# Part of the late modulation summed in the opening of a diffusion block, and filter steps ahead of the first projection

## Chip, cores and metric

The kernel runs on one core of a Trainium2 chip. The metric is the device time of one execution in microseconds (us); lower is better. The engines are TensorE (PE, with its weight loads as PEld), VectorE (DVE), ScalarE (ACT), GpSimd (POOL) and SyncE (SP, whose queue issues most DMAs). Each takes its instructions in a fixed order, and waits on semaphores for the others.

## The reference

One layer of a diffusion backbone over 1024 latent tokens of width 1024, with 256 context tokens. What matters here, cut:

```python
mod = jax.nn.silu(c) @ w_ada[i] + b_ada[i]
mod_c = jax.nn.silu(c_ctx) @ w_ada[i] + b_ada[i]
sh1, sc1, g1, sh2, sc2, g2 = jnp.split(mod[:, None, :], N_MOD, axis=-1)
hc = modulate(rmsnorm(xc, norm1_g[i]), csh1, csc1)
k_c, v_c = jnp.split(hc @ w_in[i][:, NA_WIDTH:3 * NA_WIDTH], 2, axis=-1)
h = modulate(rmsnorm(x, norm1_g[i]), sh1, sc1)
q, k, v, hv, hx1, hx2, gna, ghy = jnp.split(h @ w_in[i], IN_SPLITS, axis=-1)
y_na = neighbourhood_attention(to_heads(q), ..., na_rpb[i])
y_hy = hyena_mixer(hv, hx1, hx2, *hy_params)
x = x + g1 * gated_merge(gna, ghy, y_na, y_hy, w_na_o[i], w_hy_o[i], w_out[i])
h2 = modulate(rmsnorm(x, norm2_g[i]), sh2, sc2)
x = x + g2 * swiglu(h2, ffn_w1[i], ffn_w3[i], ffn_w2[i])
return rmsnorm(x, final_g)
```

The modulation has six parts of 1024 columns: 0 and 1 (shift and scale of the first norm) are needed at once, 2 (a gate), 3 and 4 (the second norm) and 5 (the last gate) only much later; those four are "the late modulation". hyena_mixer convolves with filters that a small network of two sine layers makes from the positions alone (hid = sin(freq * (z @ w1 + b1)), the same again with w2, then @ w3 and a decay), so they depend on no activation.

## The kernel before, in words

Everything is fp32. Products that must keep fp32 precision are made of three fast matmuls of operands split into a rounded high part and the rest: names ending in h and l (hTh, hTl, wh, wl). ACT makes the high part and DVE the low one (`split`, L178), so a matmul with hTl waits for DVE.

The kernel runs in stages: the opening, the side phase, attention with the hyena branch's output, the mixing and output projection, and the feed-forward layer's two halves. The change touches the first two.

**The opening** (`opening`, L741, fed by the generator `hidden`, L283). It computes modulation parts 0 and 1 with matmuls on 1 MB blocks (wada, ada_ps), normalizes x, transposes it on PE (hT_ps), modulates it into hT (`chunk`, or the same lines in `hidden`), and multiplies by the v columns of w_in (wv). There are three passes of eight steps: x tiles 0 to 3, x tiles 4 to 7, and the two ctx tiles (hcT). A step takes one 128-row chunk of the contraction for the four (or two) tiles, 12 (or 6) matmuls at L751, and then transposes the chunk that comes two steps later. At a pass's end the banks are copied to vst (L760), on DVE for even tiles and on ACT for odd ones. `chunk` modulates even chunks on ACT and odd ones on DVE (L276). During the second pass the filters' network (`filter_hidden`, L420) runs in two calls: two matmuls (mlp_ps, L435), seven DVE instructions for argument and range reduction (L436 to L441), and a Sin on ACT. Before the first modulation matmul, PE runs WAKE = 8 calls of a dummy matmul (awake_ps, L356).

**The side phase** (`run`, from L1110). Two generators are interleaved by `_merged`, which always takes the one that has used the smallest part of its weight: `side`, of weight SIDE = 496, and `project`, of weight 33, which makes one projection (48 matmuls in_ps of 512 columns, L199) per turn. `side` in turn merges the filters (weight 97) with `ada_rows` (weight 39), and then runs the long convolution. A filter step issues eight small matmuls (filt_ps, L464) into two banks, and DVE multiplies these by a decay (fv, L471); after four steps, a DFT of the filter follows (dft_ps). psf has five banks, so filt_ps comes to wait for the fv of two steps before. The weight split for the next projection (wl, L178) is on DVE too.

`ada_rows` (L999) computes the late modulation without PE: for each of the parts in pairs (3, 4) and (2, 5), each half of 512 columns and each of eight row blocks, it loads 256 KB of w_ada (wal, four buffers) by SP's queue and DVE adds wal times a column of silu(c) to aacc (L1017; the first of eight is a plain multiplication, L1019). Then a matmul with ones sums over the partitions (ar_ps) and DVE adds the bias row (arow). That makes 64 loads and 64 DVE instructions. After the pair (3, 4) the rows are transposed (ada_t) into mod2.

An instruction that isn't pinned (`keep_in_program_order`) can be placed by the scheduler elsewhere in its engine's order; pinned ones keep the order in which they are written.

Of the kernel before, what the change touches and what calls it, by code (L numbers as in the profile page):

```python
# [160 lines left out]
class Block:  # L161
# [258 lines left out]
    def filter_hidden(self, pool, late, psf):  # L420
        nc, a = self.nc, self.a
        hid, w3 = late()
        self.tc.keep_in_program_order(nc.sync.dma_start(w3, a["fw3"]))
# [4 lines left out]
        w1, w2, col = m[0:66, 0:P], m[:, P:2 * P], m[:, 2 * P:]
        for w, src, b, dst in ((w1, z[0:66], 0, z), (w2, z, 1, hid)):
            arg = pool.tile([P, T], F32, tag="farg", name="farg", bufs=1)  # L430
            kf = pool.tile([P, T], F32, tag="fkf", name="fkf", bufs=1)
            for h in range(2):
                sl = slice(h * 512, (h + 1) * 512)
                ps = psf.tile([P, 512], F32, tag="f", name="mlp_ps")
                self.tc.keep_in_program_order(nc.tensor.matmul(ps, w, src[:, sl], start=True, stop=True))  # L435
                nc.vector.tensor_scalar(arg[:, sl], ps, col[:, b:b + 1], col[:, 2:3], op0=ALU.add, op1=ALU.mult)  # L436
            nc.vector.tensor_scalar(kf, arg, 1.0 / TWO_PI, MAGIC, op0=ALU.mult, op1=ALU.add)
            nc.vector.tensor_scalar(kf, kf, MAGIC, None, op0=ALU.subtract)
            nc.vector.scalar_tensor_tensor(arg, kf, -C1, arg, op0=ALU.mult, op1=ALU.add)
            nc.vector.scalar_tensor_tensor(arg, kf, -C2, arg, op0=ALU.mult, op1=ALU.add)  # L440
            nc.vector.tensor_scalar(arg, arg, PI_LO, -PI_LO, op0=ALU.min, op1=ALU.max)  # L441
# [556 lines left out]

    def ada_rows(self, pool, psf):  # L999

        nc, a = self.nc, self.a
# [3 lines left out]
        def sums(r, pair):
            for n, part in enumerate(pair):
                for h in range(2):
                    acc = pool.tile([P, 512], F32, tag="aacc", name="aacc", bufs=2)  # L1010
                    for k in range(8):
                        w = pool.tile([P, 512], F32, tag="wal2", name="wal", bufs=4)
                        at = part * D + 512 * h
                        nc.sync.dma_start(w, a["w_ada"][k, :, at:at + 512])
                        c = self.cs[:, 2 * k:2 * k + 1]
                        if k:
                            nc.vector.scalar_tensor_tensor(acc, w, c, acc, op0=ALU.mult, op1=ALU.add)  # L1017
                        else:
                            nc.vector.tensor_scalar(acc, w, c, None, op0=ALU.mult)  # L1019
                        yield 0.6  # L1020
                    ps = psf.tile([P, 512], F32, tag="f", name="ar_ps")
                    for j in range(2):
                        g = 64 * h + 32 * j
                        nc.tensor.matmul(ps[g:g + 32, 0:256], ones, acc[:, 256 * j:256 * j + 256], start=True,
                                         stop=True, tile_position=(0, g))
                    rs = r[64 * h:64 * h + 64, 256 * n:256 * n + 256]
                    nc.vector.tensor_add(rs, ps[64 * h:64 * h + 64, 0:256], rs)

        for pair in ((3, 4), (2, 5)):
            r = pool.tile([P, 512], F32, tag="arow", name="arow", bufs=1)  # L1030
            nc.gpsimd.memset(r, 0.0)
            for n, part in enumerate(pair):
                for j in range(4):
                    at = part * D + 256 * j
                    nc.gpsimd.dma_start(r[32 * j:32 * j + 1, 256 * n:256 * n + 256], a["b_ada"][0:1, at:at + 256])
            yield from sums(r, pair)
            for n, part in enumerate(pair):
                for j in range(4):
                    nc.gpsimd.dma_start(self.modd[part][0:1, 256 * j:256 * j + 256],
                                        r[32 * j:32 * j + 1, 256 * n:256 * n + 256])  # L1040
            if pair[0] == 3:
                pt = psf.tile([P, 512], F32, tag="f", name="ada_t")
                for j in range(4):
                    nc.tensor.transpose(pt[:, j * P:(j + 1) * P], r[:, j * P:(j + 1) * P], self.ident)
                v = pt.rearrange("p (n h g q) -> p n q g h", n=2, h=2, g=4)[:, :, 0]
                cols = lambda t: t.rearrange("p (g h) -> p g h", h=2)
                nc.vector.tensor_copy(cols(self.mod2[:, 1, :]), v[:, 0])
                nc.vector.scalar_tensor_tensor(cols(self.mod2[:, 0, :]), v[:, 1], 1.0, cols(self.ng[:, 1, :]),
                                               op0=ALU.add, op1=ALU.mult)
# [552 lines left out]
```

## Time and profile before

| what | value |
| --- | --- |
| median of 3 runs | 1702.17 us (1702.06 to 1704.37) |
| profiled execution | 1705.87 us, of which the span is 1704.1 us |
| mean granted TensorE clock | 0.987 |
| opening, 0 to 95.5 us | PE busy 86.53 us |
| side phase, 95.5 to 607 us | PE busy 491.40 of 511.50 us, clock 0.97 |
| attention and hyena output, to 913 us | PE busy 300.93 of 306.00 us |
| mixing, to 1046 us | PE busy 131.96 of 133.00 us |
| feed-forward, to 1704 us | PE busy 644.59 of 658.00 us |

The profile shows one execution. "Busy" is the time in which an engine has an instruction running; what ended an idle stretch is inferred from semaphores. The clock is the share of full speed that was granted to TensorE: at 0.50 the same matmul takes twice as long, and PE still counts as busy. The DMA share is the mean busy share of the core's 16 DMA engines.

### The profile page before, as it was taken

How to read it: one execution, taken by the hardware profiler on the slowest of the kernel's cores; microseconds unless marked ns; L12 is line 12 of the kernel's file. 1: busy time of each engine (PE TensorE's matmuls, PEld its weight loads, DVE VectorE, ACT ScalarE, POOL GpSimd, SP SyncE). 2: the span in 40 equal slices, each digit the busy share in tenths (PEclk: the TensorE clock that was granted, in tenths of full speed). 3: DMA queues.
4: the chain of work that ended last, by engine and by line, in shares of the span. 5: the costliest groups of instructions: out<-in, count | busy, mean ns of one | idle time of the engine just before them, and what ended most of it. 6: DMA issues, size and time to landing. Idle time of an engine off the chain costs nothing.

```text
span 1704.1 us, 22676 instructions
## 1 busy us (share of the span) xinstructions
PE 1655.4 (97%) x8144; PEld 1311.7 (77%) x8144; DVE 1232.1 (72%) x2095; ACT 685.8 (40%) x1202; POOL 149.6 (9%) x271
## 2 busy tenths in 40 slices
PE   8989999999999999999999999999999999999997
PEld 5767766777767787887787887888888888778886
DVE  3756788799988876565865868967865666379477
ACT  6532343313112124555654326733333333355455
POOL 0010020101000022020200001000100111000000
PEclk9989999999999999999999999999999999999999
DMA  9265366554555365344747414333422223394344
GB/s 362 82 216 176 119 211 206 175 180 169 173 173 204 124 201 183 109 148 146 211 155 262 153 62 173 122 126 120 159 101 97 99 103 115 117 386 152 97 120 155
DMA packets 110310, 274.38 MB, mean 161 GB/s; under 512 B 15471, under 2 KB 24563, under 8 KB 107893
## 3 DMA queue, kind: packets, MB, share of 16 engines
q1 hardware_dynamic: 90296, 212.39, 37.2%
q0 software_dynamic: 19104, 60.08, 10.4%
q8 instruction: 65, 1.06, 0.3%
q10 hardware_dynamic: 797, 0.45, 0.1%
q14 instruction: 48, 0.39, 0.1%
HBM read 205.48 MB, written 67.39 MB: 160 GB/s over the span
## 4 chain that ended last, share of the span: by engine, by line
PE 55%; DVE 5%; DMA 4%; ACT 1%; issue 1%; ACTq 0%; DVEq 0%; SPq 0%
PE x_ps L1303 15%; PE z_ps L1303 7%; PE in_ps L199 6%; PE dx_ps L1472 5%; PE out_ps L1241 4%; PE dz_ps L1472 3%; PE hy_ps L199 2%; PE y_ps L1303 2%; PE pt_ps L927 2%; PE pt_ps L913 2%; PE na_ps L199 2%; PE dy_ps L1472 1%; PE s_ps L893 1%; DMA ar<-g 1%; PE s_ps L896 1%
## 5 line engine op out<-in xcount | busy, mean ns | idle before, releaser
L199 PE MATMUL in_ps<-hTh,wl 128*128 128x512 f32 x576 | 236.8, 411 | 5.1 <-ACT proj L697 4.0
L199 PE MATMUL in_ps<-hTl,wh 128*128 128x512 f32 x576 | 230.1, 399 | 0.0
L199 PE MATMUL in_ps<-hTh,wh 128*128 128x512 f32 x576 | 229.9, 399 | 0.0
L199 PEld LDWEIGHTS in_ps<-hTh,wl 128*128 128x128 f32 x576 | 110.3, 192 | 34.9 <-issue 6.5
L199 PEld LDWEIGHTS in_ps<-hTh,wh 128*128 128x128 f32 x576 | 110.1, 191 | 24.6
L199 PEld LDWEIGHTS in_ps<-hTl,wh 128*128 128x128 f32 x576 | 110.4, 192 | 23.5 <-issue 1.0
L178 DVE TENSOR_TENSOR ol<-ws,oh 128x512 fp32r<-128x512 f32 x88 | 60.4, 689 | 51.5 <-ACT oh L177 51.3
L177 ACT CAST wh<-wr 128x1024 fp32r<-128x1024 f32 (+1 forms) x60 | 52.6, 876 | 103.5 <-PE in_ps L199 83.0
L178 DVE TENSOR_TENSOR wl<-wr,wh 128x1024 fp32r<-128x1024 f32 (+1 forms) x60 | 60.3, 1006 | 44.9 <-ACT wh L177 44.7
L178 DVE TENSOR_TENSOR ol<-ar,oh 128x512 fp32r<-128x512 f32 x77 | 52.8, 688 | 49.3 <-ACT oh L177 49.3
L177 ACT CAST oh<-ar 128x512 fp32r<-128x512 f32 x77 | 47.9, 622 | 85.8 <-PE dx_ps L1472 38.8
L177 ACT CAST oh<-ws 128x512 fp32r<-128x512 f32 x88 | 54.8, 622 | 59.0 <-PE x_ps L1303 29.0
L902 ACT ACTIVATE pe<-pe,mx 128x640 f32<-128x640 f32 x64 | 52.6, 822 | 50.9 <-DVE mx L901 50.9
L1472 PE MATMUL dx_ps<-ol,oh 128*128 128x512 f32 x176 | 69.3, 394 | 1.7 <-DVE ol L178 1.7
L1472 PE MATMUL dx_ps<-oh,ol 128*128 128x512 f32 x176 | 68.1, 395 | 2.9 <-DVE ol L178 2.9
L901 DVE CUSTOM_DVE_ANT_0 pe<-s_ps,bias 128x640 f32<-128x640 f32 x64 | 50.1, 819 | 27.8 <-PE s_ps L896 27.8
L1472 PE MATMUL dx_ps<-oh 128*128 128x512 f32 x176 | 69.0, 392 | 0.0
L544 PE MATMUL dft_ps<-a,matf 128*128 128x512 f32 x128 | 65.8, 596 | 1.1 <-DMA matf<-in_dft_f 0.9
L178 DVE TENSOR_TENSOR ol<-wr,oh 128x512 fp32r<-128x512 f32 x70 | 48.1, 689 | 22.9 <-ACT oh L177 22.8
L177 ACT CAST oh<-wr 128x512 fp32r<-128x512 f32 x70 | 43.3, 622 | 52.8 <-PE x_ps L1303 16.0
L1017 DVE SCALAR_TENSOR_TENSOR aacc<-wal,cs,aacc 128x512 f32<-128x512 f32 x56 | 41.9, 747 | 19.4 <-DMA wal<-in_w_ada 18.7
L1243 DVE TENSOR_TENSOR x<-x,out_ps 128x512 f32<-128x512 f32 x64 | 42.6, 684 | 15.0 <-PE out_ps L1241 14.7
(414 smaller groups left out, 4313.1 us busy)
## 6 DMA issues: line engine op xcount, KB each, us to landing
wr<-in_w SPq DMA_DIRECT2D x52, 512.0 KB, 3.6
ar<-g SPq DMA_DIRECT2D x77, 256.0 KB, 2.9
wr<-in_w_in SPq DMA_DIRECT2D x36, 512.0 KB, 3.9
wal<-in_w_ada SPq DMA_DIRECT2D x64, 256.0 KB, 3.3
matf<-in_dft_f SPq DMA_DIRECT2D x32, 384.0 KB, 3.8
bias<-in_rpb SPq DMA_DIRECT2D x64, 192.0 KB, 3.6
g<-t POOLq DMA_DIRECT2D x47, 256.0 KB, 3.0
w<-in_w SPq DMA_DIRECT2D x44, 256.0 KB, 5.4
```

Of the source, the lines that this page charges most:

```text
L177: pin(self.nc.scalar.copy(hi, src))
L178: pin(self.nc.vector.tensor_sub(lo, src, hi.bitcast(F32)))
L199: mm = nc.tensor.matmul(ps, ww[:, k * P:(k + 1) * P], xx[:, k, pos:pos + width], start=(i == 0), stop=(i == n - 1))
L544: nc.tensor.matmul(ps, m[:, 0], v.rearrange("p a b -> p (a b)"), start=True, stop=False)
L901: nc.vector.tensor_tensor_reduce(pe, ps[:, 256:896], bt, -1.0, 3e38, ALU.add, ALU.min, mx[:, 0:1])
L902: nc.scalar.activation(pe, pe, AF.Exp, bias=mx[:, 0:1], scale=-1.0, accum_out=mx[:, 1:2])
L913: pin(nc.tensor.transpose(pt[:, at:at + P], pe[:, c * P:(c + 1) * P], self.ident))
L1017: nc.vector.scalar_tensor_tensor(acc, w, c, acc, op0=ALU.mult, op1=ALU.add)
L1241: nc.tensor.matmul(ps, gg[x][:, tk], ww[y][:, sl], start=(i == 0), stop=(i == n - 1))
L1243: nc.vector.tensor_add(x1[:, sl], x1[:, sl], ps)
L1303: mm = nc.tensor.matmul(ps, w[u][:, k * P:(k + 1) * P], x[v][:, k, :], start=(start and k == 0 and i == 0), stop=(stop and k == 3 and i == 2),
L1472: nc.tensor.matmul(ps[j], x[u][:, j * P:(j + 1) * P], w[v], start=(start and i == 0 and c == 0), stop=(stop and i == N - 1 and k == len(re ...
```

## The change

1. Parts 3 and 4 of the late modulation move from `ada_rows` into the opening, as the new generator `wide_sums`: 16 loads of 512 KB (three ahead, in the ring of buffers that held x) and 16 DVE instructions on 128x1024, pinned. Two are issued per step in steps 1 to 7 of the second pass, and one each after steps 0 and 2 of the ctx pass; ar_ps, arow and ada_t follow there. `ada_rows` keeps the pair (2, 5), 32 loads and 32 DVE instructions, now pinned, with weight 20.
2. The filters' first layer goes first: its loads (mlp, feat) stand ahead of ACT's other loads but one, its two matmuls ahead of the dummy matmuls, and its DVE steps are spread over the start and the first steps of the first pass. The second layer's matmuls come in step 7 of the second pass. WAKE goes from 8 to 5.
3. All chunks of the second and ctx passes are modulated on ACT and pinned.
4. Two steps of `side` are issued before the first projection, and SIDE goes from 496 to 477.

The diff, cut:

```diff
-SIDE = 496
+SIDE = 477
-WAKE = 8
+WAKE = 5
...
-    def chunk(self, pool, pt, n, mod, hi, lo, k, raw=None, pin=lambda i: i):
+    def chunk(self, pool, pt, n, mod, hi, lo, k, raw=None, pin=lambda i: i, plain=False):
...
-        if k % 2:
+        if k % 2 and not plain:
...
+        nc.scalar.dma_start(self.bcol, a["bcol"])
         mlp = self.filter_hidden(mp, late, psf)
-        for n in ("ng", "bcol", "cw", "times"):
+        next(mlp)
+        for n in ("ng", "cw", "times"):
...
             self.split(*(t[:, k, :] for t in hT[0]), h, inorder)
+            if k < 3:
+                next(mlp)
...
+                    sums = self.wide_sums(ring, pool, psf)
+                    next(sums)
...
             if k:
-                self.chunk(pool, turns[k], 4, self.mod1[:, 0], *hT[1], k)
+                self.chunk(pool, turns[k], 4, self.mod1[:, 0], *hT[1], k, None, inorder, True)
+                for _ in range(2):
+                    next(sums)
...
-            if k in (1, 5):
-                next(mlp)
+            if k in (1, 7):
+                for _ in range(6 if k == 7 else 1):
+                    next(mlp)
...
-            self.chunk(pool, after[k], 2, self.mod1[:, 1], hcT[0], hcT[1], k)
+            self.chunk(pool, after[k], 2, self.mod1[:, 1], hcT[0], hcT[1], k, None, inorder, True)
+            if k in (0, 2):
+                next(sums)
+            if k == 4:
+                next(sums, None)
...
+    def wide_sums(self, ring, pool, psf):
+        nc, a, pin = self.nc, self.a, self.tc.keep_in_program_order
+        pair = (3, 4)
...
+        order = [(part, k) for part in pair for k in range(8)]
+        loaded = []
+        def load():
+            part, k = order[len(loaded)]
+            loaded.append(ring("wal"))
+            pin(nc.sync.dma_start(loaded[-1], a["w_ada"][k, :, part * D:(part + 1) * D]))
+        for _ in range(3):
+            load()
+        yield
+        for i, (part, k) in enumerate(order):
+            c = self.cs[:, 2 * k:2 * k + 1]
+            if k:
+                pin(nc.vector.scalar_tensor_tensor(acc, loaded[i], c, acc, op0=ALU.mult, op1=ALU.add))
+            else:
+                acc = ring("aacc")
+                pin(nc.vector.tensor_scalar(acc, loaded[i], c, None, op0=ALU.mult))
+            if i + 3 < len(order):
+                load()
+            if k == 7:
+                for h in range(2):
+                    self.late_total(psf, r, ones, acc[:, 512 * h:512 * h + 512], part - 3, h)
+            yield
...
-        for pair in ((3, 4), (2, 5)):
+        pair = (2, 5)
...
-                        yield from _merged((fgen, 97), (self.ada_rows(fp, psf), 39))
+                        yield from _merged((fgen, 97), (self.ada_rows(fp, psf), 20))
...
+                spectra = side()
+                for _ in range(2):
+                    next(spectra)
                 next(proj)
-                for _ in _merged((side(), SIDE), (proj, 33)):
+                for _ in _merged((spectra, SIDE), (proj, 33)):
```

`late_total` is the pair of ar_ps matmuls with the addition to arow, as it stood in `ada_rows` (now one function for both callers).

How this moves instructions. First, DVE at the start of the side phase, from the last vst of the ctx pass on. Before:

```order
L760 COPY vst<-in_ps 128x512
L1019 TENSOR_SCALAR aacc<-wal,cs 128x512
L1017 SCALAR_TENSOR_TENSOR aacc<-wal,cs,aacc 128x512 x7
L1019 TENSOR_SCALAR aacc<-wal,cs 128x512
L1017 SCALAR_TENSOR_TENSOR aacc<-wal,cs,aacc 128x512 x3
L178 TENSOR_TENSOR wl<-wr,wh 128x1024
L471 SCALAR_TENSOR_TENSOR fv<-filt_ps,dec 128x2x256 x2
L477 SCALAR_TENSOR_TENSOR fv<-hb,fv 1x256
```

and after, where vst is at L783, fv at L494 and the sums of `ada_rows` at L1108 and L1110:

```order
L783 COPY vst<-in_ps 128x512
L1110 TENSOR_SCALAR aacc<-wal,cs 128x512
L494 SCALAR_TENSOR_TENSOR fv<-filt_ps,dec 128x2x256
L500 SCALAR_TENSOR_TENSOR fv<-hb,fv 1x256
L494 SCALAR_TENSOR_TENSOR fv<-filt_ps,dec 128x2x256 x3
L178 TENSOR_TENSOR wl<-wr,wh 128x1024
L494 SCALAR_TENSOR_TENSOR fv<-filt_ps,dec 128x2x256 x4
L1108 SCALAR_TENSOR_TENSOR aacc<-wal,cs,aacc 128x512
```

Twelve sums stood ahead of the first fv; now one does.

Second, DVE in the second pass, up to the arow that PE's ar_ps feeds (after; L1071 and L1074 are the wide sums, L306 and L310 the scaling of ctx, L1040 arow):

```order
L1074 TENSOR_SCALAR aacc<-wal,cs 128x1024
L1071 SCALAR_TENSOR_TENSOR aacc<-wal,cs,aacc 128x1024
L178 TENSOR_TENSOR hTl<-htmp,hTh 128x512
L1071 SCALAR_TENSOR_TENSOR aacc<-wal,cs,aacc 128x1024 x2
L178 TENSOR_TENSOR hTl<-htmp,hTh 128x512
L1071 SCALAR_TENSOR_TENSOR aacc<-wal,cs,aacc 128x1024
L306 RECIPROCAL rstd1c<-rstd1cs 128x2
L310 TENSOR_SCALAR x<-x,rstd1c 128x1024
L1071 SCALAR_TENSOR_TENSOR aacc<-wal,cs,aacc 128x1024
L310 TENSOR_SCALAR x<-x,rstd1c 128x1024
L178 TENSOR_TENSOR hTl<-htmp,hTh 128x512
L1071 SCALAR_TENSOR_TENSOR aacc<-wal,cs,aacc 128x1024 x2
```

Before, the filters' first layer and four of the modulations (L276) stood in this place, and nothing on PE but hTl and mlp_ps depended on it; now the ar_ps matmuls behind PE's step 3 wait for the last of these sums.

Third, DVE at the start of the ctx pass. Before:

```order
L439 SCALAR_TENSOR_TENSOR farg<-fkf,farg 128x1024
L276 TENSOR_SCALAR htmp<-hT_ps,mod_248 128x256
L440 SCALAR_TENSOR_TENSOR farg<-fkf,farg 128x1024
L178 TENSOR_TENSOR hcTl<-htmp,hcTh 128x256
L441 TENSOR_SCALAR farg<-farg 128x1024
L178 TENSOR_TENSOR hcTl<-htmp,hcTh 128x256
L178 TENSOR_TENSOR wl<-wr,wh 128x1024
L760 COPY vst<-in_ps 128x512 x2
```

and after (L454 to L463 are the filters' second layer):

```order
L454 TENSOR_SCALAR farg<-mlp_ps,mlp 128x512 x2
L455 TENSOR_SCALAR fkf<-farg 128x1024
L457 TENSOR_SCALAR fkf<-fkf 128x1024
L783 COPY vst<-in_ps 128x512
L459 SCALAR_TENSOR_TENSOR farg<-fkf,farg 128x1024
L783 COPY vst<-in_ps 128x512
L461 SCALAR_TENSOR_TENSOR farg<-fkf,farg 128x1024
L178 TENSOR_TENSOR hcTl<-htmp,hcTh 128x256
L463 TENSOR_SCALAR farg<-farg 128x1024
L1071 SCALAR_TENSOR_TENSOR aacc<-wal,cs,aacc 128x1024
L178 TENSOR_TENSOR hcTl<-htmp,hcTh 128x256 x2
L1071 SCALAR_TENSOR_TENSOR aacc<-wal,cs,aacc 128x1024
```

The first hcTl came before the copies of the second pass's banks; it now comes behind both and behind the wide steps of the filters' second layer.

More of the change, by code (lines that the diff above doesn't have):

```diff
@@ L349, in hidden @@
             square(j)
-        r = scaled(0, 4, "rstd1")
+        r = scaled(0, 4, "rstd1", inorder)
         for j in range(3):
-            times(xs[j], r[:, j:j + 1])
+            times(xs[j], r[:, j:j + 1], inorder)
         nc.scalar.activation(xs[3], xs[3], AF.Copy, scale=r[:, 3:4])
+        next(mlp)
         awake = psf.tile([P, 512], F32, tag="f", name="awake_ps")
@@ L393, in hidden @@
         turns = [self.turned(psf, xs[4:8], k, True) for k in range(2)]
-        self.chunk(pool, turns[0], 4, self.mod1[:, 0], *hT[1], 0, None, inorder)
+        self.chunk(pool, turns[0], 4, self.mod1[:, 0], *hT[1], 0, None, inorder, True)
         yield
@@ L406, in hidden @@
                     times(xs[8 + j], r[:, j:j + 1])
-            if k in (1, 5):
-                next(mlp)
+            if k in (1, 7):
+                for _ in range(6 if k == 7 else 1):
+                    next(mlp)
             if k == 6:
@@ L420, in filter_hidden @@
     def filter_hidden(self, pool, late, psf):
-        nc, a = self.nc, self.a
-        hid, w3 = late()
-        self.tc.keep_in_program_order(nc.sync.dma_start(w3, a["fw3"]))
+        nc, a, pin = self.nc, self.a, self.tc.keep_in_program_order
         m = pool.tile([P, 2 * P + 3], F32, name="mlp")
-        self.tc.keep_in_program_order(nc.scalar.dma_start(m, a["mlp"]))
+        nc.scalar.dma_start(m, a["mlp"])
         z = pool.tile([P, T], F32, name="feat")
-        self.tc.keep_in_program_order(nc.scalar.dma_start(z[0:66], a["feat"]))
+        nc.scalar.dma_start(z[0:66], a["feat"])
         w1, w2, col = m[0:66, 0:P], m[:, P:2 * P], m[:, 2 * P:]
-        for w, src, b, dst in ((w1, z[0:66], 0, z), (w2, z, 1, hid)):
+        for b in range(2):
+            if b:
+                hid, w3 = late()
+                nc.sync.dma_start(w3, a["fw3"])
+            w, src, dst = (w2, z, hid) if b else (w1, z[0:66], z)
+            held = (lambda i: i) if b else pin
             arg = pool.tile([P, T], F32, tag="farg", name="farg", bufs=1)
@@ L434, in filter_hidden @@
                 ps = psf.tile([P, 512], F32, tag="f", name="mlp_ps")
[L435 to L441, printed above, removed]
+                pin(nc.tensor.matmul(ps, w, src[:, sl], start=True, stop=True))
+                held(nc.vector.tensor_scalar(arg[:, sl], ps, col[:, b:b + 1], col[:, 2:3], op0=ALU.add, op1=ALU.mult))
+            held(nc.vector.tensor_scalar(kf, arg, 1.0 / TWO_PI, MAGIC, op0=ALU.mult, op1=ALU.add))
+            yield
+            held(nc.vector.tensor_scalar(kf, kf, MAGIC, None, op0=ALU.subtract))
+            yield
+            held(nc.vector.scalar_tensor_tensor(arg, kf, -C1, arg, op0=ALU.mult, op1=ALU.add))
+            yield
+            held(nc.vector.scalar_tensor_tensor(arg, kf, -C2, arg, op0=ALU.mult, op1=ALU.add))
+            yield
+            held(nc.vector.tensor_scalar(arg, arg, PI_LO, -PI_LO, op0=ALU.min, op1=ALU.max))
+            yield
             nc.scalar.activation(dst, arg, AF.Sin)
@@ L995, in hyena_out, with late_rows, late_total @@
                 yield
+    def late_rows(self, r, pair):
+        nc, a = self.nc, self.a
+        nc.gpsimd.memset(r, 0.0)
+        for n, part in enumerate(pair):
+            for j in range(4):
+                at = part * D + 256 * j
+                nc.gpsimd.dma_start(r[32 * j:32 * j + 1, 256 * n:256 * n + 256], a["b_ada"][0:1, at:at + 256])
+    def late_total(self, psf, r, ones, acc, n, h):
+        nc = self.nc
+        ps = psf.tile([P, 512], F32, tag="f", name="ar_ps")
+        for j in range(2):
+            g = 64 * h + 32 * j
+            nc.tensor.matmul(ps[g:g + 32, 0:256], ones, acc[:, 256 * j:256 * j + 256], start=True,
+                             stop=True, tile_position=(0, g))
+        rs = r[64 * h:64 * h + 64, 256 * n:256 * n + 256]
+        nc.vector.tensor_add(rs, ps[64 * h:64 * h + 64, 0:256], rs)
@@ new lines, in late_store @@
+    def late_store(self, r, pair):
+        for n, part in enumerate(pair):
+            for j in range(4):
+                self.nc.gpsimd.dma_start(self.modd[part][0:1, 256 * j:256 * j + 256],
+                                         r[32 * j:32 * j + 1, 256 * n:256 * n + 256])
+    def wide_sums(self, ring, pool, psf):
+        nc, a, pin = self.nc, self.a, self.tc.keep_in_program_order
+        pair = (3, 4)
+        ones = pool.tile([P, 32], F32, name="ones")
+        nc.gpsimd.memset(ones, 1.0)
+        r = pool.tile([P, 512], F32, name="arow")
+        self.late_rows(r, pair)
+        order = [(part, k) for part in pair for k in range(8)]
[6 more added lines that the diff above has]
+            load()
+        yield
+        for i, (part, k) in enumerate(order):
[10 more added lines that the diff above has]
+                    self.late_total(psf, r, ones, acc[:, 512 * h:512 * h + 512], part - 3, h)
+            yield
+        self.late_store(r, pair)
+        pt = psf.tile([P, 512], F32, tag="f", name="ada_t")
+        for j in range(4):
+            nc.tensor.transpose(pt[:, j * P:(j + 1) * P], r[:, j * P:(j + 1) * P], self.ident)
+        v = pt.rearrange("p (n h g q) -> p n q g h", n=2, h=2, g=4)[:, :, 0]
+        cols = lambda t: t.rearrange("p (g h) -> p g h", h=2)
+        nc.vector.tensor_copy(cols(self.mod2[:, 1, :]), v[:, 0])
+        nc.vector.scalar_tensor_tensor(cols(self.mod2[:, 0, :]), v[:, 1], 1.0, cols(self.ng[:, 1, :]),
+                                       op0=ALU.add, op1=ALU.mult)
@@ L999, in ada_rows @@
     def ada_rows(self, pool, psf):
-        nc, a = self.nc, self.a
+        nc, a, pin = self.nc, self.a, self.tc.keep_in_program_order
+        pair = (2, 5)
         ones = pool.tile([P, 32], F32, name="ones", tag="ones", bufs=1)
         nc.gpsimd.memset(ones, 1.0)
[L1007 to L1027, printed above, removed]
@@ L1029, in ada_rows @@
-        for pair in ((3, 4), (2, 5)):
[L1030 to L1049, printed above, removed]
@@ new lines, in ada_rows @@
+        r = pool.tile([P, 512], F32, tag="arow", name="arow", bufs=1)
+        self.late_rows(r, pair)
+        for n, part in enumerate(pair):
+            for h in range(2):
+                acc = pool.tile([P, 512], F32, tag="aacc", name="aacc", bufs=2)
+                for k in range(8):
+                    w = pool.tile([P, 512], F32, tag="wal2", name="wal", bufs=4)
+                    at = part * D + 512 * h
+                    nc.sync.dma_start(w, a["w_ada"][k, :, at:at + 512])
+                    c = self.cs[:, 2 * k:2 * k + 1]
+                    if k:
+                        pin(nc.vector.scalar_tensor_tensor(acc, w, c, acc, op0=ALU.mult, op1=ALU.add))
+                    else:
+                        pin(nc.vector.tensor_scalar(acc, w, c, None, op0=ALU.mult))
+                    yield 0.6
+                self.late_total(psf, r, ones, acc, n, h)
@@ L1053, in run @@
+        self.late_store(r, pair)
     def run(self):
```

## The prediction

> **What bounds the kernel now.** I read the page first.
>
> ```profile
> span 1704.1 us, 22676 instructions
> PE 1655.4 (97%) x8144; PEld 1311.7 (77%) x8144; DVE 1232.1 (72%) x2095; ACT 685.8 (40%) x1202; POOL 149.6 (9%) x271
> ```
>
> TensorE (PE) is busy for 1655.4 of 1704.1 us, so only 48.7 us of idle time can be won, plus whatever PE does at a lowered clock. The windows by stage say where that is (columns: us, then PE, PEld, DVE, ACT, POOL busy, granted clock, DMA share, GB/s).
>
> ```profile
> 0.00:95.50 95.50, 86.53 (x504) 63.04 (x505) 50.51 (x94) 54.56 (x94) 5.13 (x14) 1.00 0.55 214
> 95.50:607.00 511.50, 491.40 (x2096) 368.27 (x2095) 423.60 (x686) 137.50 (x226) 46.88 (x80) 0.97 0.52 174
> ```
>
> The opening idles 9.0 us, nearly all before its first matmul. The side phase idles 20.1 us and is the one with a clock of 0.97; VectorE (DVE) is busy 83% of it, against 53% in the opening. PE's waits name the cause.
>
> ```profile
> PE filt_ps L464 <- DVE fv L471: 13.9, 4, 7.2
> PE awake_ps L356 <- DVE csp L289: 5.3, 1, 5.3
> PE dft_ps L544 <- DMA matf<-in_dft_f: 0.9, 1, 0.9
> ```
>
> The four waits of filt_ps on fv are these (PE's timeline; the bracket is the idle time ahead and who ended it):
>
> ```profile
> 119.48 2.08 PE L464 MATMUL filt_ps<-fw,hid 64*128 64x256 f32 x8 [7.17 <-DVE fv L471]
> 235.40 2.07 PE L464 MATMUL filt_ps<-fw,hid 64*128 64x256 f32 x6 [2.99 <-DVE fv L471]
> 283.52 1.29 PE L464 MATMUL filt_ps<-fw,hid 64*128 64x256 f32 x8 [2.83 <-DVE fv L471]
> 285.70 2.07 PE L464 MATMUL filt_ps<-fw,hid 64*128 64x256 f32 x6 [0.89 <-DVE fv L471]
> ```
>
> But fv itself takes 0.6 us. DVE's timeline shows what it stands behind:
>
> ```profile
> 114.67 0.75 DVE L1017 SCALAR_TENSOR_TENSOR aacc<-wal,cs,aacc 128x512 f32<-128x512 f32 x1 [2.09 <-DMA wal<-in_w_ada]
> 116.94 0.75 DVE L1017 SCALAR_TENSOR_TENSOR aacc<-wal,cs,aacc 128x512 f32<-128x512 f32 x1 [1.52 <-DMA wal<-in_w_ada]
> 117.61 1.22 DVE L178 TENSOR_TENSOR wl<-wr,wh 128x1024 fp32r<-128x1024 f32 x1
> 118.74 1.28 DVE L471 SCALAR_TENSOR_TENSOR fv<-filt_ps,dec 128x512 f32<-128x512 f32 x2
> ...
> 281.99 0.75 DVE L1017 SCALAR_TENSOR_TENSOR aacc<-wal,cs,aacc 128x512 f32<-128x512 f32 x1 [3.71 <-DMA wal<-in_w_ada]
> ```
>
> DVE works in order, and the sums of the late modulation ahead of fv wait for their own loads. So PE waits through DVE for a 256 KB transfer. Behind each of these gaps PE runs slowly (columns: us, PE busy, granted clock, DMA share, GB/s):
>
> ```profile
> 120.00:125.00 5.00, 5.00 (x17) 0.50 0.69 207
> 125.00:130.00 5.00, 5.00 (x17) 0.67 0.37 109
> ...
> 235.00:240.00 5.00, 4.60 (x12) 0.50 0.61 209
> 240.00:245.00 5.00, 5.00 (x21) 0.91 0.54 157
> ...
> 285.00:290.00 5.00, 4.30 (x11) 0.53 0.68 229
> 290.00:295.00 5.00, 5.00 (x19) 0.79 0.40 111
> ```
>
> **The change part by part.** The sum is made against the profiled execution's 1705.87 us, 3.70 above the median of 1702.17; I carry the difference over to the median.
>
> *Taken away in the side phase.* The idle time: 7.17 + 2.99 + 2.83 + 0.89 = 13.9, and with dft_ps's 0.9 (a load late in the same busy queues) 14.8 us. The clock: in 120–130 PE does 5 x 0.50 + 5 x 0.33 = 4.15 us less work than at full clock; in 235–245 4.60 x 0.50 + 5 x 0.09 = 2.75; in 285–295 4.30 x 0.47 + 5 x 0.21 = 3.05. That is 10.0, in all 24.8 us. What remains of the sums there is half the loads (32 of 64) and half the instructions, spread over the same filter steps, and all eight fv of the first group now stand behind a single sum, not behind twelve. I take 80% as gone, since only the later gaps can still meet a late load: **−19.8**. The lower end is half (−12.4: one sum between fv's can still wait on a late load), the upper all of it.
>
> *Filter layer 1.* Its two matmuls leave the second pass:
>
> ```profile
> 57.98 1.88 PE L435 MATMUL mlp_ps<-feat,mlp 66*128 66x512 f32 x4
> 59.30 0.80 PE L751 MATMUL in_ps<-wl,hTh 128*128 128x512 f32 x1
> ...
> 82.91 0.38 PE L261 MATMUL hT_ps<-ident,x 128*128 128x128 f32 x2
> ```
>
> From 57.98 to 59.30 they hold PE for 1.3 us there, and at the start PE is idle or warming up (the 5.3 us above): **−1.3**. Its DVE steps and its Sin move into the first pass, where neither is full:
>
> ```profile
> 20.00:40.00 20.00, 20.00 (x154) 14.01 (x157) 7.87 (x19) 12.04 (x22) 0.00 (x0) 1.00 0.95 384
> ```
>
> DVE is busy 7.87 of 20 us there; a table load for Sin on ACT is covered by ACT's idle time there (12.04 of 20 us busy). If that cover fails, each load costs the 1.28 us of
>
> ```profile
> 2.62 1.28 ACT L217 ACT_TABLE_LOAD   x1 [2.62 <-issue]
> ```
>
> *The start.*
>
> ```profile
> 9.37 1.06 ACT L300 ACTIVATE junk<-x 128x1024 f32<-128x1024 f32 x1 [0.32 <-DMA x<-in_x]
> 11.83 1.07 PE L233 MATMUL ada_ps<-wada,csp 128*32 128x256 f32 x16 [1.15 <-DMA wada<-in_w_ada]
> ```
>
> The first modulation matmul waits for its weights. 0.4 MB (mlp 128x259 and feat 66x1024, four bytes each) now goes first; at the 384 GB/s of that row it is 1.05 us later for all that follows: **+1.1** (0 if those bytes fill a quiet first stretch, 2 if the two queues share badly).
>
> *Sixteen wide sums in the opening.* No row shows this instruction; nearest is the same operation on the same 128x1024 (L439). From the groups of DVE between 45 and 100 us (busy, then mean ns):
>
> ```profile
> L178 DVE TENSOR_TENSOR hTl<-htmp,hTh 128x512 fp32r<-128x512 f32 x10 | 6.9, 687 | 2.8 <-ACT hTh L177 2.7
> L178 DVE TENSOR_TENSOR hcTl<-htmp,hcTh 128x256 fp32r<-128x256 f32 x8 | 3.4, 423 | 2.9 <-ACT hcTh L177 2.9
> L760 DVE COPY vst<-in_ps 128x512 f32<-128x512 f32 x5 | 3.3, 685 | 2.5 <-PE in_ps L751 2.5
> L439 DVE SCALAR_TENSOR_TENSOR farg<-fkf,farg 128x1024 f32<-128x1024 f32 x2 | 2.4, 1222 | 0.0
> L310 DVE TENSOR_SCALAR x<-x,rstd1c 128x1024 f32<-128x1024 f32 x2 | 1.5, 747 | 0.0
> ```
>
> They are on the path in two places.
> Stall A: after step 3 of the second pass PE's ar_ps needs the eighth sum. DVE must do, from
>
> ```profile
> 53.92 1.28 DVE L760 COPY vst<-in_ps 128x512 f32<-128x512 f32 x2
> ...
> 69.70 0.69 DVE L178 TENSOR_TENSOR hTl<-htmp,hTh 128x512 fp32r<-128x512 f32 x1 [0.91 <-ACT hTh L177]
> ```
>
> on: 2 copies (1.4), 4 hTl (2.7), the first sum (0.75 as L310), seven more (8.6), two scalings of x (1.5): 15.0 us, so 68.9, and 69.8 with one wait for ACT like the 0.91 quoted. PE gets there at 57.98 (end of step 0) plus three steps of 3.2 us (59.30 to 82.91 less 1.3 for the other mlp pair, by 7) = 67.5. So PE waits 1.4 to 2.3 us, and a late load adds to it: **+2.4** (1.4 to 5).
> Stall B: the start of the ctx pass, now with a burst of DVE work ahead of its first hcTl.
> After the last step the DVE order has vst, a wide step (1.22), vst, a wide step, hcTl: 0.69 + 1.22 + 0.69 + 1.22 + 0.42 = 4.2 us. A bank is done some 0.7 us before the last matmul and the four matmuls with hcTh (0.9) come first, so PE waits 2.6; then hcTl after clip and the fifteenth sum 0.7, and ar_ps behind the sixteenth 1.2: **+4.5** (2 to 6).
> Their clock: the gaps of 2.83 and 2.99 us above each went with a clock of 0.50 and a loss of about 3 us. Two gaps of 2.4 and 2.6 could each do this or neither: **+3** (0 to 6).
> The Trainium skill says in "TensorE: Matmul & The Clock Gate", section "HAM oscillation — how this bites in real kernels", that the rule is no PE-idle gaps over about 3.4 us; by it the two new gaps would cost no clock and the sum would be 3 us lower. The trace speaks against it: 2.83 and 2.99 us were enough here, and the measurement decides.
>
> *Neutral.* All chunks on ACT: ACT is busy 54.56 of 95.5 us there. The ar_ps and ada_t matmuls and the projection that shifts into the attention loop are moved at the same length. DVE gives back 32 x 0.75 = 24 us in the side phase, which is not its bound once the loads are on time.
>
> Sum: −19.8 − 1.3 + 1.1 + 2.4 + 4.5 + 3 = −10.1; 1705.87 becomes 1695.8, the median **1692.1**. About 0.2% (3.4 us) is what a measurement of this kernel can tell from no change.
>
> **The rivals.**
> *A, nothing new stalls the clock and all side stalls go.* For: half the loads in a phase whose stalls were all late wal loads. Against: some DVE sums still stand among fv's. −24.8 − 1.3 + 1.1 + 2.4 + 4.5 = −18.1: 1684.1.
> *C, it does only half of what it says:* the remaining sums still wait for loads with fv behind them at 235 and 285. For: the order there has the sums still between fv's, and pinned now. Against: half the density. −12.4 + 9.7 (the other terms as above) = −2.7: 1699.5, within 0.2%.
> *B, slower: the wide loads are late.* Three of 512 KB are in flight in the opening, where 512 KB loads took long while it was busy, and short later:
>
> ```profile
> wal<-in_w_ada SPq DMA_DIRECT2D x64, 256.0 KB, 3.3
> x<-in_x SPq DMA_DIRECT2D x16, 512.0 KB, 7.2
> wr<-in_wv SPq DMA_DIRECT2D x4, 512.0 KB, 8.9
> ```
>
> At 7.2 us a sum comes every (7.2 + 1.22) / 3 = 2.8 us, where two per step of 3.2 need 1.6; hTl stands behind them, so the 13 sums that are loaded as slots come free cost 13 x 1.2 = 15.6 us: −10.1 + 15.6 = +5.5, 1707.7. It decides from a landing time of (1.6 + 10.1/13) x 3 − 1.22 = 5.9 us on. Against: from 40 us on the queues are nearly empty,
>
> ```profile
> 60.00:80.00 20.00, 20.00 (x96) 15.87 (x95) 17.29 (x25) 10.43 (x17) 0.00 (x0) 1.00 0.15 52
> ```
>
> at 0.15 and 52 GB/s; sixteen loads there add some 8.4 MB over 40 us, 210 GB/s, below the 384 seen.
>
> **How the numbers follow.** Forecast 0.42 (1687 to 1697), A 0.25, C 0.15, B 0.18. Faster by over 0.2%: forecast and A, 0.67; within 0.2%: C, 0.15; slower: B, 0.18. The range takes in the forecast, A with 4.1 us below it and C with 3.5 above it, and leaves B out: 1680 to 1703.
>
> **What would show it.** Right: no wait of filt_ps on fv over 1 us and a clock of 1.00 in 115–130; waits of ar_ps on aacc of 1.5 to 5 us in the second pass, and of in_ps on hcTl of 2 to 3 at the start of ctx; the mlp pair before the warm-up. Wrong: filt_ps still waits several us (C); DVE idle on wal in the opening, with PE waiting on hTl at step after step (B); or a stretch after 607 us that differs by more than 2 us, which I hold unchanged.

## The result, and the profile after

| kernel | median | runs | ratio to before, 95% interval |
| --- | --- | --- | --- |
| before | 1702.35 us | 1702.06 to 1704.37, 4 | 1 |
| changed | 1694.62 us | 1691.63 to 1695.81, 4 | 0.9949, 0.9932 to 0.9967 |

The change makes the kernel 7.7 us faster, where 10.1 were forecast. The profiled execution of the changed kernel took 1691.63 us (span 1689.9), 14.2 less than that of before; but it is the fastest of its kind, and that of before was 3.5 us over its median. So places and sizes of stalls are read from the two traces, the total from the medians.

PE's waits in the changed kernel (engine, what waits, who is waited for: total, times, longest):

```profile
PE mlp_ps L453 <- DMA feat<-in_feat: 7.5, 1, 7.5
PE ar_ps L1037 <- DVE aacc L1071: 4.9, 2, 4.1
...
PE in_ps L199 <- ACT proj L743: 2.7, 2, 2.0
...
PE in_ps L774 <- ACT hcTh L177: 2.2, 1, 2.2
...
PE filt_ps L487 <- DVE fv L494: 0.6, 2, 0.3
...
PE in_ps L774 <- DVE hcTl L178: 0.3, 1, 0.3
```

The wait of filt_ps on fv is nearly gone (13.9 to 0.6 us), and new waits stand in the opening. The windows of the changed kernel's opening and side phase (us, PE, PEld, DVE, ACT, POOL busy, granted clock, DMA share, GB/s):

```profile
0.00:107.90 107.90, 91.52 (x518) 64.67 (x518) 65.72 (x109) 61.97 (x104) 13.61 (x32) 0.97 0.73 268
107.90:590.00 482.10, 473.17 (x2064) 356.30 (x2064) 405.39 (x659) 135.98 (x225) 38.09 (x63) 1.00 0.51 169
```

The side phase now runs at a clock of 1.00 and idles 8.9 us instead of 20.1. (Its two windows don't end at the same instruction: the last DFT matmul starts at 608.5 us before and at 582.7 after. So only idle time and clock are compared here, not the length.) The opening idles 16.4 us instead of 9.0, at 0.97 instead of 1.00. Where, PE's timeline of the changed kernel says:

```profile
7.51 3.75 PE L453 MATMUL mlp_ps<-feat,mlp 66*128 66x512 f32 x4 [7.51 <-DMA feat<-in_feat]
11.19 3.21 PE L359 MATMUL awake_ps<-csp 128*32 128x256 f32 x9
...
73.28 1.08 PE L1037 MATMUL ar_ps<-aacc,ones 128*32 128x256 f32 x8 [4.06 <-DVE aacc L1071]
...
92.93 0.50 PE L774 MATMUL in_ps<-wl,hcTh 128*128 128x512 f32 x1 [2.18 <-ACT hcTh L177]
...
97.57 0.64 PE L1037 MATMUL ar_ps<-aacc,ones 128*32 128x256 f32 x8 [0.80 <-DVE aacc L1071]
```

Its windows round the two stalls (us, PE busy, clock, DMA share, GB/s) show that only the first cost clock:

```profile
70.00:75.00 5.00, 1.72 (x12) 0.64 0.77 245
75.00:80.00 5.00, 5.00 (x19) 0.67 0.69 207
...
90.00:95.00 5.00, 2.82 (x15) 1.00 0.53 197
95.00:100.00 5.00, 3.95 (x25) 1.00 0.12 31
```

The loss behind the first is 1.72 x 0.36 + 5 x 0.33 = 2.3 us. DVE at the start of the changed side phase shows the new order at work:

```profile
112.81 0.49 DVE L1110 TENSOR_SCALAR aacc<-wal,cs 128x512 f32<-128x512 f32 x1 [4.25 <-DMA wal<-in_w_ada]
114.67 0.69 DVE L494 SCALAR_TENSOR_TENSOR fv<-filt_ps,dec 128x512 f32<-128x512 f32 x1 [1.37 <-ACT dec L482]
...
126.29 1.28 DVE L494 SCALAR_TENSOR_TENSOR fv<-filt_ps,dec 128x512 f32<-128x512 f32 x2
...
129.42 0.74 DVE L1108 SCALAR_TENSOR_TENSOR aacc<-wal,cs,aacc 128x512 f32<-128x512 f32 x1
```

One sum waits for its load here, and the first fv, with 1.4 us of idle time ahead of it, waits for the decay that ACT makes (dec), not for a sum. The next sum comes 17 us later.

The opening's end is read from the last copy of a bank to vst (groups of one tile: times shortest, median, longest in ns; first and last start). Before, then changed:

```profile
L760 DVE COPY vst<-in_ps x5: 680/681/691, 53.9 to 95.6; 128x512 f32<-128x512 f32 x5
```

```profile
L783 DVE COPY vst<-in_ps x5: 681/684/692, 55.7 to 107.9; 128x512 f32<-128x512 f32 x5
```

The opening is 12.3 us longer, and the whole gains nevertheless. The rest of the study asks whether these 12.3 us buy the gain of the side phase.

### The profile page after: what moved, and what is told of

It is laid out like the page before. It is cut to its first block, busy times and chain, and to the rows that moved or that the text cites. A ratio compares the mean times of both kernels' runs of the same rounds, so it can differ in the third digit from the quotient of the medians.

```text
span 1689.9 us, 22639 instructions
## 1 busy us (share of the span) xinstructions
PE 1642.8 (97%) x8138; PEld 1302.1 (77%) x8138; DVE 1224.6 (72%) x2071; ACT 697.9 (41%) x1216; POOL 149.1 (9%) x272
## 3 DMA queue, kind: packets, MB, share of 16 engines
q8 instruction: 65, 1.06, 0.3%
## 4 chain that ended last, share of the span: by engine, by line
PE 74%; issue 9%; DVE 9%; DMA 5%; ACT 2%; POOL 1%; SPq 0%; DVEq 0%; POOLq 0%; ACTq 0%
PE x_ps L1368 15%; PE in_ps L199 12%; PE z_ps L1368 7%; PE dx_ps L1537 6%; PE out_ps L1306 4%; PE dz_ps L1537 3%; PE dft_ps L567 3%; PE hy_ps L199 3%; PE in_ps L774 2%; PE y_ps L1368 2%; PE pt_ps L936 2%; PE pt_ps L950 2%; PE na_ps L199 2%; PE dft_ps L568 2%; PE dft_ps L569 2%
## 5 line engine op out<-in xcount | busy, mean ns | idle before, releaser
L199 PE MATMUL in_ps<-hTh,wl 128*128 128x512 f32 x576 | 232.3, 403 | 4.1 <-ACT proj L743 2.7
L610 ACT COPY bp<-dft_ps 128x512 f32<-128x512 f32 x16 | 9.4, 586 | 113.4 <-PE dft_ps L569 106.0
```

The lines of the kernel that those rows point to most:

```text
L199: mm = nc.tensor.matmul(ps, ww[:, k * P:(k + 1) * P], xx[:, k, pos:pos + width], start=(i == 0), stop=(i == n - 1))
```

## The experiments

Theory "bytes", that of the prediction: the waits of the side phase come from 64 loads and the sums behind them, so half of the sums has to leave the phase. Rival "order": they come from where the sums stand among DVE's instructions; then the sums in the opening are a pure cost.

**The changed kernel again (r1).** 

> The changed kernel once more, to have its spread beside the kernels of this call. Expected 1692 to 1696 us, ratio to the kernel before 0.9935 to 0.9965. If its runs differ among themselves by the granted clock, the mean clock of a run should go with its time: 0.002 of the clock is 3.4 us.

Measured: 1694.32 us (1692.73 to 1701.05, 9 runs), ratio 0.9959 (0.9945 to 0.9972). The longest execution had the lowest mean clock, 0.991 against 0.993 to 0.995 for the others; of the kernel before, beside it, the longest (1705.84) had 0.986 and the shortest (1696.44) 0.994. Below 3 us time and clock don't go together.

**Order and pins alone (e1).** The edits to the kernel before:

```diff
+                spectra = side()
+                for _ in range(2):
+                    next(spectra)
                 next(proj)
-                for _ in _merged((side(), SIDE), (proj, 33)):
+                for _ in _merged((spectra, SIDE), (proj, 33)):
...
-                            nc.vector.scalar_tensor_tensor(acc, w, c, acc, op0=ALU.mult, op1=ALU.add)
+                            self.tc.keep_in_program_order(nc.vector.scalar_tensor_tensor(acc, w, c, acc, op0=ALU.mult, op1=ALU.add))
```

(and the same for the first of eight sums.) 

> The kernel before with two edits alone: two filter steps are issued ahead of the first projection, and the 64 late sums of the side phase keep the written order (so that they stand one at a time between the filter steps, not twelve ahead of the first). The opening is that of before. Theory 'bytes': what hurt were 64 loads of 256 KB and what is queued behind them, and half of it must leave the phase; then about half of the 24.8 us goes, 1688 to 1692 us, with a wait of filt_ps on fv of 2 us or more near 235 and 285 us. Rival 'order': the place of the sums alone made the waits; then 18 to 25 us go, 1678 to 1684 us, faster than the changed kernel by 10, and the sums in the opening are a pure cost.

Measured: 1684.65 us, ratio 0.9898 (0.9882 to 0.9914). 18 us go with all 64 loads still in the phase, and the kernel is 10 us faster than the changed one. The time is 0.65 us above the range of "order" and 3.4 below that of "bytes". The sign that "bytes" named is absent: filt_ps waits 1.4 us on fv in all, 0.6 at most. So "order" holds, near the small end of its gain.

**The sums back in the side phase (e2).** The changed kernel without `wide_sums`, with `ada_rows` for both pairs (pinned), weight 39, SIDE = 496:

```diff
-SIDE = 477
+SIDE = 496
...
-                    sums = self.wide_sums(ring, pool, psf)
-                    next(sums)
...
-                for _ in range(2):
-                    next(sums)
...
-                        yield from _merged((fgen, 97), (self.ada_rows(fp, psf), 20))
+                        yield from _merged((fgen, 97), (self.ada_rows(fp, psf), 39))
```

> The changed kernel with the 16 wide sums taken out of the opening: all 64 sums are in the side phase again, in written order, with the weights of before (39 and 496). The filters' first layer still goes first, the chunks stay on ScalarE. Theory 'bytes': the opening gains some 11 us (stalls 4.1, 2.3 of clock, 3.2, and the ar_ps matmuls), the side phase loses 12 or more: 1694 to 1700 us. Rival 'order': the side phase loses under 3 us, so 1682 to 1688 us.

Measured: 1685.55 us, ratio 0.9904 (0.9888 to 0.992), as the rival said: at this weight the filters' first layer, the chunks and WAKE, which set it apart from e1, cost 0.9 us.

**The first total later (e3).**

```diff
-            if k == 7:
+            if i in (LATE, 15):
+                n = i // 15
                 for h in range(2):
-                    self.late_total(psf, r, ones, acc[:, 512 * h:512 * h + 512], part - 3, h)
+                    self.late_total(psf, r, ones, kept[n][:, 512 * h:512 * h + 512], n, h)
```

with LATE = 11, and the first accumulator in a buffer of its own (the scratch of the last squares moves to make room). 

> The changed kernel with the first total over the partitions (ar_ps of part 3) issued four sums later, after step 5 of the second pass, so TensorE doesn't wait for the eighth sum after step 3. Theory: the wait of 4.1 us and the clock loss of 2.3 us behind it go, but VectorE is the bound of the second pass (two wide sums and an hTl are 3.3 us per step of 3.1), so the wait at the start of the ctx pass grows by 2 to 4: 1690 to 1693 us for a changed kernel at 1694.6. Rival: the wait was only a matter of that one place; all 6.3 us go: 1688 to 1689 us.

Measured: 1692.11 us, ratio 0.9942 (0.9926 to 0.9957), 2.2 us under the changed kernel (r1). Its timeline and windows at the start of the ctx pass:

```profile
88.18 0.77 PE L775 MATMUL in_ps<-wl,hcTh 128*128 128x512 f32 x1 [1.70 <-DVE vst L784]
90.76 1.22 PE L775 MATMUL in_ps<-wh,hcTl 128*128 128x512 f32 x2 [0.53 <-DVE hcTl L179]
```

```profile
85.00:90.00 5.00, 3.15 (x10) 0.82 0.44 170
90.00:95.00 5.00, 4.47 (x11) 0.50 0.30 112
```

The 4.06 us after step 3 are gone. The time is in the range that the theory gave, but not for its reason: the waits at the start of the ctx pass don't grow (1.70, 0.53 and 0.37 us, where the changed kernel has 2.18, 0.26 and 0.80). What comes back is clock. It now falls to 0.50 behind the next stall, which it had not done, and that is 3.15 x 0.18 + 4.47 x 0.50 = 2.8 us.

**The merge weight (e4).** SIDE = 477 on the kernel of e1:

```diff
-SIDE = 496
+SIDE = 477
```

> The kernel of e1_order_and_pins with SIDE = 477 in place of 496, the last part of the change that can be had without the sums in the opening. In e1's trace the largest wait left is 5.6 us of in_ps on proj near 535 us with the clock at 0.76 and 0.90 behind it; in the changed kernel (477) the same kind of wait is 2.0 at most. Theory: the merge weight moves that projection away from the load that it waits for, so 3 to 7 us go, and 1 to 3 come back in the attention stage (pt_ps on yrow and na_ps on wl, 3 us longer in the changed kernel): 1679 to 1684 us, the fastest so far. Rival: the weight only moves the waits about; 1684 to 1688 us.

Measured: 1677.35 us (1675.26 to 1678.67), ratio 0.9844 (0.9828 to 0.986): the fastest kernel here, 25 us under before and 17 under the changed one, with none of its opening. In e1's trace a projection waits for a late load of the convolution by way of ACT (PE's timeline, then the window behind it):

```profile
536.50 0.79 PE L199 MATMUL in_ps<-hTh,wl 128*128 128x512 f32 x1 [5.59 <-ACT proj L720]
```

```profile
535.00:540.00 5.00, 3.50 (x8) 0.51 0.56 228
```

and in e4's that stretch is full:

```profile
490.00:600.00 110.00, 109.56 (x447) 1.00 0.45 156
```

**Each half of e1 by itself.** First the two early steps without pins (e5: the first hunk of e1's diff). 

> The kernel before with the two filter steps ahead of the first projection alone, the sums not pinned. Fourteen sums then stand in VectorE's order between the second fv and the third. Theory 'order by pins': the stall stays, between the first two filter steps and the third: 1695 to 1703 us. Rival: the two early steps are what removes it; 1683 to 1688 us.

Measured: 1696.77 us, ratio 0.9966 (0.9954 to 0.9978). The stall has moved to the third filter step, and filt_ps waits 15.3 us on fv in all, more than the 13.9 of before. What this kernel gains doesn't come from there; its trace lacks the wait of 4.0 us on proj that before has. (The profiled execution is the longest of its eleven, 1701.06 us.) PE, then DVE:

```profile
122.04 2.07 PE L464 MATMUL filt_ps<-fw,hid 64*128 64x256 f32 x6 [8.60 <-DVE fv L471]
```

```profile
113.37 0.75 DVE L1017 SCALAR_TENSOR_TENSOR aacc<-wal,cs,aacc 128x512 f32<-128x512 f32 x1 [2.82 <-DMA wal<-in_w_ada]
117.06 3.19 DVE L1017 SCALAR_TENSOR_TENSOR aacc<-wal,cs,aacc 128x512 f32<-128x512 f32 x4 [2.94 <-DMA wal<-in_w_ada]
120.17 1.22 DVE L178 TENSOR_TENSOR wl<-wr,wh 128x1024 fp32r<-128x1024 f32 x1
121.30 1.28 DVE L471 SCALAR_TENSOR_TENSOR fv<-filt_ps,dec 128x512 f32<-128x512 f32 x2
```

Then the pins without the early steps (e6: the second hunk). 

> The kernel before with the 64 late sums kept in written order, and nothing else. Theory 'order by pins': this one edit gives nearly all of what e1 gave (17.9 us): 1683 to 1689 us. Rival: the two early filter steps are needed as well, since the first projection otherwise runs into them: 1690 to 1697 us.

Measured: 1687.46 us, ratio 0.9905 (0.989 to 0.992), 15 us by one edit. PE's wait of 13.9 us on fv is now

```profile
PE filt_ps L464 <- DVE fv L471: 2.0, 4, 0.6
```

and DVE at the same place:

```profile
112.04 1.28 DVE L471 SCALAR_TENSOR_TENSOR fv<-filt_ps,dec 128x512 f32<-128x512 f32 x2
113.24 0.48 DVE L1019 TENSOR_SCALAR aacc<-wal,cs 128x512 f32<-128x512 f32 x1
113.76 0.69 DVE L471 SCALAR_TENSOR_TENSOR fv<-filt_ps,dec 128x512 f32<-128x512 f32 x1
```

No sum waits here (in the whole trace one does, for 1.9 us): each is placed after an fv, and its load has landed by then. The pins also change the order of loads in SP's queue (two loads of matf now stand ahead of the fifth wal); no run takes the two orders apart. The groups of L1017 in the whole trace (count | busy, mean ns | idle time before them, what ended most of it) show the difference, before and in e4, with the same 64 loads:

```profile
L1017 DVE SCALAR_TENSOR_TENSOR aacc<-wal,cs,aacc 128x512 f32<-128x512 f32 x56 | 41.9, 747 | 19.4 <-DMA wal<-in_w_ada 18.7
```

```profile
L1017 DVE SCALAR_TENSOR_TENSOR aacc<-wal,cs,aacc 128x512 f32<-128x512 f32 x56 | 41.7, 744 | 2.3 <-DMA wal<-in_w_ada 2.2
```

**Parts 3 and 4 left out (e7).** The kernel of e2 without these sums, weight 20:

```diff
-                    sums = self.wide_sums(ring, pool, psf)
-                    next(sums)
+                    nc.gpsimd.memset(self.mod2.rearrange("p a b -> p (a b)"), 0.5)
```

> The kernel of e2_sums_back with the sums of parts 3 and 4 left out altogether (no load, no sum, no total; the second norm's modulation is set to constants), weights 20 and 496. It shows what the 32 sums cost where they are in e2. Theory 'order': once they stand one at a time among the filter steps they cost nothing: within 3 us of e2's 1685.6. Theory 'bytes' (all that is left of it): half of the sums still costs several us there: 1676 to 1681 us.

Measured: 1678.08 us, ratio 0.9849 (0.9832 to 0.9865). By its range this is the outcome of "bytes". But its trace lacks the wait of 5.4 us of in_ps on proj that e2 has, as e4's does; with the weight of 20 that meeting doesn't occur. Against e8, below, which has all sums and no such meeting either, it is 3 us faster. As the two also differ in SIDE (496 and 477), that is an estimate of the price of 32 sums in the side phase and not a measurement; some cost of their number isn't excluded.

**The price of the opening (e8).** The kernel of e2 with SIDE = 477, that is the changed kernel less its first part:

```diff
-SIDE = 496
+SIDE = 477
```

> The changed kernel with nothing undone but its first part: all 64 late sums in the side phase, in written order with weight 39, and SIDE = 477 as in the changed kernel. Against the changed kernel (1694.4 us) it gives the price of the sixteen wide sums in the opening. Theory 'pure cost': the opening is shorter by the 12 us that the trace shows less what the filters' first layer does at the start, and the side phase loses nothing: 1677 to 1682 us. Rival: the two moves belong together, and 64 sums beside an earlier schedule cost several us: 1684 to 1690 us.

Measured: 1681.13 us, ratio 0.9871 (0.9858 to 0.9885). So at SIDE = 477 the sixteen wide sums cost the changed kernel 1694.4 − 1681.1 = 13.3 us. And e8 is 3.8 us above e4, which differs from it by the filters' first layer, the chunks, WAKE and a few pins in the opening alone: that part costs too at this weight. Openings of e4 and of e8:

```profile
L760 DVE COPY vst<-in_ps x5: 680/685/692, 53.7 to 95.3; 128x512 f32<-128x512 f32 x5
```

```profile
L775 DVE COPY vst<-in_ps x5: 681/684/692, 56.1 to 99.4; 128x512 f32<-128x512 f32 x5
```

4.1 us, of which 2.4 lie ahead of the first vst. PE's start in e8:

```profile
8.02 3.75 PE L445 MATMUL mlp_ps<-feat,mlp 66*128 66x512 f32 x4 [8.02 <-DMA feat<-in_feat]
11.70 3.21 PE L359 MATMUL awake_ps<-csp 128*32 128x256 f32 x9
14.54 0.42 PE L233 MATMUL ada_ps<-wada,csp 128*32 128x256 f32 x3
```

The two matmuls wait for feat, and as the first work on PE they hold it for 3.7 us (8.02 to 11.70), where they held it for 1.3 in the second pass before; the dummy matmuls and ada_ps queue behind them.

**The square closed (e10).** The changed kernel with the other weight:

```diff
-SIDE = 477
+SIDE = 496
```

> The changed kernel with SIDE = 496 in place of 477. It closes the square of two places for the sums (opening, side phase) and two weights. Theory: the weight decides where a projection meets the late load of the convolution, whatever the place of the sums, so 496 costs the 5 to 9 us here that it cost between e4 and e1: 1699 to 1703 us. Rival: the meeting hangs on the exact order and doesn't occur here: 1692 to 1696 us.

Measured: 1689.91 us, ratio 0.9924 (0.9912 to 0.9937), below the ranges of both. The theory falls: with the sums in the opening 496 is the better weight, by 4.5 us, while without them 477 is, by 7.3 (e1 to e4) and 4.4 (e2 to e8). Its waits hold no meeting at all:

```profile
PE in_ps L199 <- ACT proj L743: 0.5, 1, 0.5
```

What a weight gives hangs on the exact order that it makes. So does the price of the wide sums: at 496 it is 1689.9 − 1685.6 = 4.4 us (e10 against e2) and not 13.3, and the intervals of the two ratios overlap (0.9912 to 0.9937 and 0.9888 to 0.9920), so it may be less. The last vst starts 11.3 us later than in e2 (110.9 and 99.6), but e2 has the meeting of 5.4 us with its loss of clock, and e10 doesn't. The sums in the opening win at neither weight.

**A smaller weight (e9).** On e4's kernel:

```diff
-SIDE = 477
+SIDE = 458
```

 

> The kernel of e4_side_477 with SIDE = 458. Theory: past the one meeting that 477 avoids there is nothing more to win by the weight: 1676 to 1683 us. Rival: the earlier the side phase ends, the better; 1671 to 1675 us.

Measured: 1681.1 us, ratio 0.987 (0.9854 to 0.9885), 3.7 above e4: nothing more to win that way, as the theory had it. A projection meets a late load again, near 654 us:

```profile
654.26 0.80 PE L199 MATMUL in_ps<-hTh,wl 128*128 128x512 f32 x1 [1.98 <-ACT proj L720]
```

```profile
654.00:657.00 3.00, 2.74 (x7) 0.51 0.48 188
```

## Why the prediction was right, and where its steps were not

The direction was right and the size near. Most of the signs that it named came: filt_ps waits 0.3 us on fv at most, the clock is 1.00 from 115 to 130 us, ar_ps waits 4.1 us, and the filters' pair comes first. But four steps had the wrong size (the side phase, the filters' first layer, both stalls), the first of them also the wrong reason, and that their errors cancelled is luck.

- *The side phase, −19.8.* In the traces na_ps starts at 913.0 before and at 899.8 after, 13.2 us earlier with an opening 12.3 longer: −25.5. The stalls of filt_ps went whole, 13.3 us of idle time and the 10.0 of clock. New waits of dft_ps, 4.8 us where 0.9 stood, took back 3.9, which makes −19.4 for what the step counted; its 80% came out through a wait that it didn't name. (By their medians e6 and e1 put early steps and pins at 15 and 18 us.) Another 4 us come from the wait of in_ps on proj with its clock, which I left out as it was not to change. That failed: the new weight and order moved it. Before it was one wait, with a loss of 6.05 x 0.17 + 10 x 0.18 = 2.8 us in its two windows (us, PE busy, clock, DMA share, GB/s):

```profile
PE in_ps L199 <- ACT proj L697: 4.0, 1, 4.0
```

```profile
480.00:490.00 10.00, 6.05 (x23) 0.83 0.50 174
490.00:500.00 10.00, 10.00 (x32) 0.82 0.37 111
```

  and after it is 2.7 us in two pieces, with a clock of 1.00. The matmuls that moved to the opening (ar_ps, ada_t) are part of the rest.
- *Its reason.* "Half the loads" was counted as the cause. e6 falsifies it: a gain of 15 us comes with all 64 loads in place, from pinning the sums so that they no longer stand twelve deep ahead of fv. The second reason that the step gave, that all eight fv stand behind a single sum, was the right one.
- *The filters' first layer and the start, −1.3 and +1.1.* Together with the chunks, not −0.2 but +3.8 at SIDE = 477 (e8 against e4) and +0.9 at 496 (e2 against e1). The step "at the start PE is idle or warming up" failed: the pair took 3.75 us there, and the modulation weights had landed before PE was through (ada_ps waited 0.2 us for them, against 2.2 before).
- *Stall A, +2.4 and up to 5:* 4.1. The missing part is what the step left open, late loads: DVE waited 1.5 and 0.4 us for wal there. From the issues of transfers (count, size, median us to landing):

```profile
wal<-in_w_ada SPq DMA_DIRECT2D x16, 512.0 KB, 4.5
```

  4.5 us is under the 5.9 from which rival B decides, so B didn't come, though some loads were late.
- *Stall B, +4.5:* 2.2 + 0.3 + 0.8 = 3.3. The wait of 2.2 us ended with ACT's hcTh and not with DVE's hcTl, where I had named DVE alone: ACT copies two banks, modulates the chunk and splits a weight first. The forecast sign, a wait of in_ps on hcTl of 2 to 3 us, didn't come (0.3).
- *The clock, +3:* 2.3, all behind A. After 2.18 us the clock stayed at 1.00. The step read too much into the gap of 2.83 us: a second one of 0.89 follows it, and the clock was still 1.00 between the two (283.5 to 285 us).
- *After 607 us,* held unchanged within 2 us: it was not. From the last DFT matmul to na_ps PE idles 6.5 us instead of 5.1, as pt_ps waits longer for yrow (4.3 us in all instead of 2.8). From na_ps to the first feed-forward matmul it takes 139.7 us instead of 138.2, as na_ps waits 2.3 us for wl instead of 0.4. Together that is 3.0 us, and r1's trace, of its longest execution, has more (142.4 us for the second stretch). So one of the signs of being wrong came. The feed-forward takes 650.4 us instead of 652.9, but it was not edited, and in r1 it takes 654.2: that is the spread of executions.
- Moved matmuls (ar_ps, ada_t), called neutral, are among the opening's 12.3 us.

So the forecast came out near because a larger gain in the side phase met a larger cost in the opening. In medians, along the runs at SIDE = 477: early steps, pins and weight give 25 (e4), the filters' first layer and the chunks take back 3.8 (e8), and the sums in the opening 13.3; what is left is the change's 8. Along the runs at 496 the same 8 come apart otherwise: early steps and pins give 18 (e1), the first layer and the chunks take back 0.9 (e2), the sums in the opening 4.4 (e10), and the weight 4.5. The gain of the pins and the cost of the opening stand on both ways, the size of the cost doesn't.

That the wide sums cost 13.3 at 477 where the opening is only 107.9 − 99.4 = 8.5 longer than e8's can be followed in the two traces. From the last vst to na_ps they take 791.9 and 791.5 us, from there to the feed-forward 139.7 and 137.4. The rest is that the profiled execution of the changed kernel is some 3 us under its median. So in these two traces the departure of half the sums gave nothing to the stages behind the opening.

## What to carry to other kernels

When an engine that works in order holds two kinds of work, one that others wait for and one that waits for loads, look at the order before the amount: here a pin that put each load-bound instruction behind the urgent one gave 15 us, while moving half of that work to another stage cost 4 to 13 there. Before filler work goes into a stage, add up what its engine holds per step of the bound engine; here two wide sums and an hTl take 3.2 us (2 x 1.28 + 0.69), a whole step of PE. And try the parts of a change apart: here one edit (the pins, 15 us) gave twice the whole. A decomposition by single runs holds for the order in which the parts were added; here the weight turned 13.3 into 4.4.

## What the runs showed of the hardware

The granted clock falls after short idle times of TensorE, and not always: 2.99 us (before), 1.98 us (e9) and 1.70 us (e3) went with 0.50 or 0.51, while 2.18 us (changed) left 1.00. No single threshold fits these. The Trainium skill ("TensorE: Matmul & The Clock Gate", section "HAM oscillation — how this bites in real kernels") gives gaps over about 3.4 us; the runs here show losses well below that. Also, the first matmuls of the filters' network, as the first work on PE, took 1.06 us each (the first 1.19) where the same ones took 0.59 us each in the second pass before, in a window whose granted clock is shown as 1.00.
